# Holding ScalarE's weight casts and exponentials behind product copies and query squares in a two-layer attention and pooling block

## The chip, the cores and the metric

The kernel runs on one core of a Trainium2 chip. The metric is the device time of one execution in microseconds (us). Kernels are compared as medians of runs on the same chip. A profile of one execution gives the span, from the first instruction to the last, and what each engine did in it: PE is TensorE (matmuls), PEld its weight loads, DVE is VectorE, ACT is ScalarE, POOL is GpSimd, SP is SyncE, which here only issues DMAs.

## The reference

Two layers of the same block over 528 tokens (16 learned ones ahead of 512) of width 1024, in fp32, batch 1. Cut to what matters:

```python
def hybrid_layer(x, norm_g, w_in, ..., w_a, w_b, w_out, cos, sin, k_top):
    h = rms_norm(x, norm_g)
    proj = jnp.einsum('btd,de->bte', h, w_in)
    q, k, v, gate_a, u_b, gate_b, q_idx, k_idx, w_idx, merge = jnp.split(...)
    q = apply_rope(rms_norm(q...), cos_h, sin_h)        # k too; q_idx, k_idx: rope alone
    attn = indexer_sparse_attention(q, k, v, q_idx, k_idx, w_idx, k_top)
    y_a = jnp.einsum('bte,ed->btd', attn * jax.nn.silu(gate_a), w_a)
    pooled = multiscale_pool(u_b, pool_w, pool_b, pool_s)
    y_b = jnp.einsum('bte,ed->btd', pooled * jax.nn.silu(gate_b), w_b)
    g_a, g_b = jnp.split(jax.nn.sigmoid(merge), 2, axis=-1)
    return x + jnp.einsum('btd,de->bte', g_a * y_a + g_b * y_b, w_out)
```

The attention has 8 heads of 64 over one key and value head. For each query an index score picks the 128 best of the keys that its chunk may see, and a softmax runs over these alone. The output is the last 512 tokens after both layers.

## The kernel before

**Products in split fp32.** A weight matrix and an activation matrix are each split into a high part, rounded to the matmul type `fp32r`, and a low part, the rest. A product takes three passes on TensorE: high by high, high by low and low by high. Weights come in 54 chunks (27 a layer), mostly of 256 columns. SP loads each chunk as two halves into `raw` tiles (four buffers, so two chunks at a time), and each half is prepared into tiles `w` (eight buffers), in one of three ways:

- `high` and `low`: a ScalarE cast and a VectorE subtraction.
- `minus` and `plus` (the chunks in `by_dma`, lines 217 to 230): for the low part ScalarE writes the negated cast (L220), and a DMA from POOL's queue adds the raw weights to it in place (L221). The high part is another cast (L225). These are the chunks of the pools, the queries and `w_b` in each layer, and two of `w_out` in the last.
- `mixed_prep` (the chunks in `mixed`, lines 254 to 318): the ten gate chunks of each layer and the last two of `w_out`. Their products use seven multiplications of quarter blocks in place of eight, so the weights are first summed in blocks: `hi(n)` is a ScalarE cast (L264), `lo(n)` a VectorE subtraction (L267), and two DMAs on POOL's queue add blocks (L251, L278). Nine steps, `i0` to `i8`, make the seven operands `a12`, `a11`, `s2`, `s1`, `s3`, `s4`, `a22`.

**The order of the work.** TensorE and VectorE run in the order in which the code issues their instructions (`manual_schedule`). ScalarE, POOL and SP are ordered by the compiler's scheduler, which issues what it finds ready first; `tc.issue_after(ins)` forces what its block issues on the engine of `ins` to stand behind `ins` in that engine's order, with no wait for its end. Preparation steps wait in a queue: `group_done`, called after each group of matmuls, runs what is due and then one step, and `chunk()` runs all that are left before a chunk is used. In the mixed products `end()` runs them by a count, with a lead of five steps (`LEAD`) and nine steps for seven products; `NEEDS` gives the step that must be done before an operand's product.

**The places that the change touches.**

- `hi` puts its cast behind `mark[0]` where there is a mark. Before the change, only `rows` in the last stage sets one (L1483).
- `queries(g)` makes the query projection in four groups of 24 matmuls (128 tokens each, in a PSUM bank `d`, of which there are three). After a group, `q_post` issues two VectorE products for the rotation (tiles `t1`, `t2`), a ScalarE square for the norm (`sq`, L660), and a POOL addition (L669). The same `group_done` then runs the next preparation step, so `minus` of the next chunk is issued right after a square.
- `group_of_products` runs the seven products of a mixed chunk (12 matmuls each). `out` copies three of them from PSUM by ScalarE (`p1`, `u2`, `p5`, L1010). VectorE adds them to other products, and the bank of `p1` and `p5` is written again by a later product.
- `attention` runs beside the mixed products: `soft` computes on VectorE the logits and the minimum `mn`, and on ScalarE the exponential of each head (L782).
- In the last stage of layer 1 `rows` multiplies the first half of `w_out` by tokens, and `mix_out` runs the two mixed chunks of the second half, with `turned_out` to bring the results out.

Of the kernel before, what the change touches and what calls it, by code (L numbers as in the profile page):

```python
# [10 lines left out]
AF = mybir.ActivationFunctionType  # L11
# [9 lines left out]
HD = 64  # L21
# [70 lines left out]
def tile_block(ctx: ExitStack, tc: tile.TileContext, x, meta, w_in, pool_w, w_a, w_b, w_out, rows, hgain, c_tab, out):  # L92
    nc = tc.nc
    act, gp = nc.scalar, nc.gpsimd
# [20 lines left out]
    chunks = []  # L115
# [22 lines left out]
    raws, ready = {}, {}  # L138
# [37 lines left out]
    def w_prep_enqueue(casts_first=False, after=None):  # L176
        c = W["prep"]
        if c >= len(chunks):
            return
        W["prep"] += 1  # L180
        kt = chunks[c][0][0].shape[1]
        cols = 2048 // kt
        if c in plain:
            return
        ready[c] = {}
        if c in mixed:
            prep_q.extend(mixed_prep(c))
            return
        parts = ready[c] = ([], [])

        def split(which):
            if c == kept_chunk:
                if which not in own:
                    own[which] = one.tile([128, KT, 256], F32R, tag=("Ahi", "Alo")[which], name="wo")
                i = len(parts[which])
                t = own[which][:, i:i + kt // 2, :]
            else:
                t = w_tile().rearrange("p (k e) -> p k e", e=cols)
            parts[which].extend(t[:, k] for k in range(kt // 2))
            return t  # L200

        his, own = {}, {}

        def high(s):
            his[s] = split(0)
            act.copy(his[s], raws[c][s])

        def low(s):
            dve.tensor_sub(split(1), raws[c][s], f(his[s]))
            if s == 1:  # L210
                del raws[c]
                w_load()

        def second():
            low(0)
            high(1)

        def minus(s):
            t = split(1)
            act.activation(t, raws[c][s], AF.Copy, scale=-1.0)  # L220
            gp.dma_start(t, raws[c][s], accum_op=OP.add)  # L221

        def plus(s):
            t = split(0)
            act.copy(t, raws[c][s])  # L225
            if s == 1:
                del raws[c]
                w_load()
                with tc.issue_after(added[0]):
                    first_sum(c + 1)  # L230

        def highs():
            with tc.issue_after(after) if after else nullcontext():
                high(0)
                high(1)

        if casts_first:
            prep_q.extend((highs, lambda: low(0), lambda: low(1)))
        elif c in by_dma:
            prep_q.extend((lambda: minus(0), lambda: minus(1), lambda: plus(0)))  # L240
            if c in metas:
                prep_q.append(lambda: meta_queries(metas[c], raws[c]))
            prep_q.append(lambda: plus(1))
        else:
            prep_q.extend((lambda: high(0), second, lambda: low(1)))

    added, mark = [None], [None]

    def first_sum(c):
        if c in mixed:  # L250
            gp.dma_start(raws[c][0][:, 1], raws[c][0][:, 0], accum_op=OP.add)  # L251

    def mixed_prep(c):

        r0, r1 = raws[c]
        blk = {"a11": r0[:, 0], "a21": r0[:, 1], "a12": r1[:, 0], "a22": r1[:, 1]}
        src = {"a11": "a11", "a12": "a12", "a22": "a22", "s3": "a21", "s2": "s2", "s1": "a11", "s4": "a12"}
        ops = ready[c]

        def hi(n):  # L260
            t = w_tile().rearrange("p (s k e) -> p s k e", s=2, k=4)
            ops[n] = t
            with tc.issue_after(mark[0]) if mark[0] else nullcontext():
                act.copy(t[:, 0], blk[src[n]])  # L264

        def lo(n):
            dve.tensor_sub(ops[n][:, 1], blk[src[n]], f(ops[n][:, 0]))  # L267

        def i0():
            hi("a12")  # L270
            hi("a11")

        def i1():
            lo("a12")
            blk["s2"] = tmp.tile([128, 544], F32, tag="L", name="s2", bufs=LB)[:, :512].rearrange(
                "p (k e) -> p k e", k=4)
            dve.tensor_add(blk["s2"], blk["a21"], blk["a22"])
            gp.dma_start(blk["a12"], blk["s2"], accum_op=OP.add)  # L278
            lo("a11")

        def i2():
            dve.tensor_sub(blk["a11"], blk["s2"], blk["a11"])

        def i3():
            hi("s2")

        def i4():
            lo("s2")
            hi("s1")

        def i5():
            lo("s1")
            hi("s3")

        def i6():
            lo("s3")
            hi("s4")
            first_sum(c + 1)

        def i7():  # L300
            lo("s4")
            hi("a22")

        def i8():
            lo("a22")
            del raws[c]
            w_load()

        def counted(fn):
            def item():  # L310
                fn()
                progress[c] += 1
            return item

        progress[c] = 0
        return [counted(fn) for fn in (i0, i1, i2, i3, i4, i5, i6, i7, i8)]
# [138 lines left out]
    NR = one.tile([128, 4, NH], F32, name="NR")  # L455
# [192 lines left out]
    def q_post(t, ps, normed, dst, g=0):  # L648
        s, m = TOK[t]
        p3 = ps[:m, :256].rearrange("p (h d) -> p h d", h=4)  # L650
        t1 = tmp.tile([128, HB], F32, tag="tt", name="t1", bufs=6)
        t2 = tmp.tile([128, HB], F32, tag="tt", name="t2", bufs=6)
        v1 = t1[:m, :256].rearrange("p (h d) -> p h d", h=4)
        C, S = (Cg[:m, t], Sg[:m, t]) if normed else (ctab[:m, t], stab[:m, t])
        dve.tensor_tensor(v1, p3, C[:, None, :].to_broadcast([m, 4, 64]), op=OP.mult)
        dve.tensor_tensor(t2[:m, :256].rearrange("p (h a d) -> p h a d", h=4, a=2), swapped(ps[:m, :256], 4),
                          S.rearrange("p (a d) -> p a d", a=2)[:, None, :, :].to_broadcast([m, 4, 2, 32]), op=OP.mult)
        if normed:
            sq = tmp.tile([128, HB], F32, tag="tt", name="sq", bufs=6)
            act.activation(sq[:m, :256], ps[:m, :256], AF.Square, scale=HD ** -0.5)  # L660
            ss = small(4, "ss4")
            rq = small(4, "rq")

        def norms():
            dve.tensor_reduce(ss[:m], sq[:m, :256].rearrange("p (h d) -> p h d", h=4), axis=AX.X, op=OP.add)
            inv_rms(rq[:m] if t == 0 else RQ[:, t - 1, 4 * g:4 * g + 4], ss[:m], dve)
        if normed and t == 0:
            norms()
        added[0] = gp.tensor_tensor(t1[:m, :256], t1[:m, :256], t2[:m, :256], op=OP.add).ins  # L669
        if normed:  # L670
            qs = tmp.tile([128, 544], F32R, tag="L", name="qs", bufs=LB)[:, :512].rearrange("p (h c) -> p h c", h=4)
        else:
            qs = tmp.tile([128, 4, 128], F32R, tag="P", name="qs", bufs=PB)

        def second():
            if normed and t == 0:
                dve.tensor_tensor(v1, v1, rq[:m, :, None].to_broadcast([m, 4, 64]), op=OP.mult)
            act.copy(qs[:m, :, 0:64], v1)
            if normed and t:
                norms()  # L680

        def third():
            dve.tensor_sub(qs[:m, :, 64:128], v1, f(qs[:m, :, 0:64]))

        def trans():
            tp = bank("a", F32R)
            for h in range(4):
                pe.transpose(tp[:, h * 128:h * 128 + m], qs[:m, h, :], identr[:m, :m])
            act.copy(dst, f(tp).rearrange("p (h c) -> p h c", h=4)[:, :, :m])
        later(second, 1)  # L690
        later(third, QN if normed else QI)
        later(trans, QN + 1 if normed else QI + 1)
# [55 lines left out]
    def attention(ensure, later_rate, on):  # L748
# [18 lines left out]
        def soft(u):  # L767
            i, j = divmod(u, 4)
            n = NK[i]
# [9 lines left out]
            dve.tensor_tensor(mn, mn, RQ[:, i, 2 * j:2 * j + 2], op=OP.mult)  # L779
            for hh in range(2):  # L780
                h = 2 * j + hh
                act.activation(L[hh][:, :n], L[hh][:, :n], AF.Exp, scale=NR[:, i, h:h + 1], bias=mn[:, hh:hh + 1],  # L782
                               accum_out=sm[:, hh:hh + 1])
            st[u] = L, sm

        def scale(u):
# [191 lines left out]
        return early, late, last_sum, operands  # L978

    ROLES = [(0, 1, 2), (2, 0, 1), (1, 2, 0)]  # L980
    NEEDS = {"a11": 1, "a12": 2, "s2": 4, "s1": 5, "s3": 6, "s4": 7, "a22": 8}

    def group_of_products(r, base, n2, operands, total, direct, mid=None):

# [22 lines left out]

        def out(ps, name):
            o = sheet(n2, name)[:, :n2]
            act.copy(o, ps[:, :n2])  # L1010
            return o

        product(U, "a11", True)
# [552 lines left out]
```

## Time and profile before

| | |
|---|---|
| time, median of 3 runs | 745.1 us (743.18 to 748.33) |
| the profiled execution's own time | 743.89 us |
| its span | 742.1 us |
| granted TensorE clock | 1.0 |
| DMA | 106.42 MB, 143 GB/s on average |

A row of the profile names the source line, the engine, the operation, what is written and read (`out<-in`), the shapes, and times. TensorE's and VectorE's instructions are all recorded by one helper and stand under L63, so there the tiles' names tell them apart: `d`, `a` and `v` are PSUM banks, `w` prepared weights, `raw` staged ones. In a row of the timeline the first number is the start in us from the span's start and the second the duration; `x` counts the instructions merged into the row, and a bracket gives the engine's idle time before it and what ended that. In a row of waits stand the total in us, how many there were, and the longest.

### The profile page before, as it was taken

The numbers are of one execution on the slowest core, as the hardware profiler recorded it, in microseconds if no ns is written. First come the engines' busy times: TensorE is split into PE (matmuls) and PEld (weight loads), VectorE is DVE, ScalarE is ACT, GpSimd is POOL, SyncE is SP. The second block draws the span as 40 slices with busy tenths as digits, with TensorE's granted clock in tenths as the row PEclk, the third lists the DMA queues.
The fourth block names the chain that finished last, engine by engine and source line by source line (L and its number), as shares of the span: only waits on it lengthen the run. The fifth ranks groups of instructions, "written<-read, shape, count | busy, mean of one in ns | idle before, by whom it ended". The sixth has DMA issues, their size and how long they took to land.

```text
span 742.1 us, 16064 instructions
## 1 busy us (share of the span) xinstructions
PE 732.4 (99%) x5949; PEld 705.6 (95%) x5949; DVE 589.4 (79%) x1500; ACT 480.8 (65%) x1099; POOL 242.6 (33%) x320
## 2 busy tenths in 40 slices
PE   8999999999999999999999999999999999999997
PEld 7999998999999999999999989998899999999997
DVE  6866999999897775894358668999989878668773
ACT  6769735657788785543245796367578878865642
POOL 3742174721221210163256411755031221106300
PEclk9999999999999999999999999999999999999999
DMA  8766764864554532633422687569464644448832
GB/s 265 231 170 162 166 145 114 225 147 100 139 119 116 127 74 85 213 118 124 135 88 86 175 179 194 150 142 201 99 159 100 160 97 93 122 116 250 197 85 69
DMA packets 103567, 106.42 MB, mean 143 GB/s; under 512 B 5008, under 2 KB 83632, under 8 KB 103488
## 3 DMA queue, kind: packets, MB, share of 16 engines
q1 hardware_dynamic: 91888, 74.89, 33.3%
q0 software_dynamic: 11520, 30.41, 22.9%
q8 instruction: 47, 0.77, 0.4%
q14 instruction: 32, 0.26, 0.1%
q10 hardware_dynamic: 80, 0.08, 0.0%
HBM read 66.41 MB, written 8.55 MB: 101 GB/s over the span
## 4 chain that ended last, share of the span: by engine, by line
PE 69%; DVE 20%; ACT 3%; DMA 2%; issue 2%; POOL 2%; SPq 1%; DVEq 0%; POOLq 0%; ACTq 0%
PE d L63 56%; PE a L63 9%; DVE sc L63 6%; PE v L63 4%; DVE m L63 4%; DVE t L63 2%; DMA xt<-in_x_dram 2%; DVE w L63 1%; DVE nf L63 1%; DVE silb L63 1%; DVE us L63 1%; DVE mlo L63 1%; ACT w L225 1%; DVE qs L63 1%; ACT lt L782 1%
## 5 line engine op out<-in xcount | busy, mean ns | idle before, releaser
L63 PE MATMUL d<-hhi,w 128*128 128x256 f32 (+3 forms) x1392 | 278.3, 291 | 0.5 <-ACT p L1010 0.5
L63 PEld LDWEIGHTS d<-hhi,w 128*128 128x128 f32 x1392 | 222.3, 188 | 3.6 <-ACT p L1010 0.7
L63 PE MATMUL d<-hlo,w 128*128 128x256 f32 (+3 forms) x696 | 189.8, 289 | 0.0
L63 PEld LDWEIGHTS d<-hlo,w 128*128 128x128 f32 x696 | 131.3, 189 | 1.4 <-issue 0.2
L63 DVE TENSOR_TENSOR w<-raw,w 128x512 fp32r<-128x512 f32 (+1 forms) x156 | 120.6, 784 | 6.5 <-ACT w L264 6.3
L63 PE MATMUL d<-hsum,w 128*128 128x264 f32 (+1 forms) x720 | 95.7, 285 | 0.4 <-ACT u L1010 0.3
L63 PEld LDWEIGHTS d<-hsum,w 128*128 128x128 f32 x720 | 89.6, 188 | 1.5 <-ACT u L1010 0.5
L63 PE MATMUL d<-w,hhi 128*128 128x256 f32 x576 | 86.2, 287 | 0.7 <-ACT sq L660 0.7
L264 ACT CAST w<-raw 128x512 fp32r<-128x512 f32 x132 | 77.0, 622 | 5.9 <-DMA raw<-s 3.2
L63 PEld LDWEIGHTS d<-w,hhi 128*128 128x128 f32 x576 | 74.7, 188 | 5.2 <-issue 2.3
L251 POOL DMA_DIRECT2D raw<-raw x22 | 19.9, 903 | 114.6 <-DMA raw<-in_w_in_dram 43.3
L221 POOL DMA_DIRECT2D w<-raw x34 | 31.5, 944 | 73.8 <-ACT w L220 51.1
L63 DVE MATCH_REPLACE8 sc<-m,sc 128x400 f32<-128x400 f32 (+2 forms) x100 | 54.4, 547 | 0.0
L63 DVE MAX8 m<-sc 128x8 f32<-128x400 f32 (+2 forms) x100 | 53.1, 556 | 0.9
L782 ACT ACTIVATE lt<-lt,mn,NR 128x144 f32<-128x144 f32 (+3 forms) x64 | 42.2, 663 | 14.2 <-DVE mn L63 13.9
L278 POOL DMA_DIRECT2D raw<-s x22 | 19.2, 871 | 90.8 <-DVE s L63 51.2
L63 DVE SCALAR_TENSOR_TENSOR sc<-r,wsg,sc 128x144 f32<-128x144 f32 (+3 forms) x56 | 32.4, 581 | 17.4 <-ACT r L706 15.0
L63 PE MATMUL d<-w,hlo 128*128 128x256 f32 x288 | 45.5, 281 | 0.0
L63 PE MATMUL d<-mhi,w 128*128 128x272 f32 (+2 forms) x192 | 45.3, 324 | 0.0
L669 POOL TENSOR_TENSOR t<-t,t 128x256 f32<-128x256 f32 (+1 forms) x34 | 32.5, 956 | 26.4 <-DVE t L63 25.0
L1411 POOL TENSOR_TENSOR hlo<-ta,hhi 128x256 fp32r<-128x256 f32 (+1 forms) x28 | 26.8, 967 | 43.6 <-PE d L63 31.4
L706 ACT ACTIVATE r<-a,wab 128x272 f32<-128x272 f32 (+2 forms) x80 | 35.7, 495 | 5.9 <-PE a L63 5.9
(245 smaller groups left out, 1548.3 us busy)
## 6 DMA issues: line engine op xcount, KB each, us to landing
raw<-in_w_in_dram SPq DMA_DIRECT2D x88, 256.0 KB, 3.4
w<-raw POOLq DMA_DIRECT2D x34, 512.0 KB, 5.9
raw<-in_w_in_dram SPq DMA_DIRECT2D x32, 512.0 KB, 4.3
raw<-in_w_out_dram SPq DMA_DIRECT2D x12, 512.0 KB, 4.0
raw<-raw POOLq DMA_DIRECT2D x22, 256.0 KB, 4.0
raw<-s POOLq DMA_DIRECT2D x22, 256.0 KB, 3.3
kept<-res SPq DMA_DIRECT2D x16, 264.0 KB, 4.7
res<-kept SPq DMA_DIRECT2D x16, 264.0 KB, 5.9
```

Of the source, the lines that this page charges most:

```text
L63: return fn(*a, **k)
L221: gp.dma_start(t, raws[c][s], accum_op=OP.add)
L225: act.copy(t, raws[c][s])
L251: gp.dma_start(raws[c][0][:, 1], raws[c][0][:, 0], accum_op=OP.add)
L264: act.copy(t[:, 0], blk[src[n]])
L278: gp.dma_start(blk["a12"], blk["s2"], accum_op=OP.add)
L669: added[0] = gp.tensor_tensor(t1[:m, :256], t1[:m, :256], t2[:m, :256], op=OP.add).ins
L706: act.activation(r[:, n - 1::-1] if i == 0 else r[:, o:o + e], ps[:, :e], AF.Relu, scale=wab[:, i, h:h + 1])
L782: act.activation(L[hh][:, :n], L[hh][:, :n], AF.Exp, scale=NR[:, i, h:h + 1], bias=mn[:, hh:hh + 1], accum_out=sm[:, hh:hh + 1])
L1411: pool_end = gp.tensor_sub(hlo[:, j, a:a + n], d, f(hhi[:, j, a:a + n]))
```

## The change

Three things are edited. `mark[0]` is now also set by the square of a query group (L660) and by each product copy (L1010). The casts of `minus` and the exponentials of `soft` are put behind the latest mark, as the casts of `hi` were already; the casts of `plus`, and of `high`, are not. And for the last chunk of all, `hi("a11")` and `lo("a11")` are issued one step later each, with `NEEDS["a11"]` raised from 1 to 2 for every chunk.

```diff
         def minus(s):
             t = split(1)
-            act.activation(t, raws[c][s], AF.Copy, scale=-1.0)
+            with marked():
+                act.activation(t, raws[c][s], AF.Copy, scale=-1.0)
             gp.dma_start(t, raws[c][s], accum_op=OP.add)
...
+    def marked():
+
+        return tc.issue_after(mark[0]) if mark[0] else nullcontext()
...
+        soon = c <= len(chunks) - 2
 
         def hi(n):
             t = w_tile().rearrange("p (s k e) -> p s k e", s=2, k=4)
             ops[n] = t
-            with tc.issue_after(mark[0]) if mark[0] else nullcontext():
+            with marked():
                 act.copy(t[:, 0], blk[src[n]])
...
         def i0():
             hi("a12")
-            hi("a11")
+            if soon:
+                hi("a11")
...
             gp.dma_start(blk["a12"], blk["s2"], accum_op=OP.add)
-            lo("a11")
+            (lo if soon else hi)("a11")
 
         def i2():
+            if not soon:
+                lo("a11")
             dve.tensor_sub(blk["a11"], blk["s2"], blk["a11"])
...
-            act.activation(sq[:m, :256], ps[:m, :256], AF.Square, scale=HD ** -0.5)
+            mark[0] = act.activation(sq[:m, :256], ps[:m, :256], AF.Square, scale=HD ** -0.5).ins
...
-                act.activation(L[hh][:, :n], L[hh][:, :n], AF.Exp, scale=NR[:, i, h:h + 1], bias=mn[:, hh:hh + 1],
-                               accum_out=sm[:, hh:hh + 1])
+                with marked():
+                    act.activation(L[hh][:, :n], L[hh][:, :n], AF.Exp, scale=NR[:, i, h:h + 1], bias=mn[:, hh:hh + 1],
+                                   accum_out=sm[:, hh:hh + 1])
...
-    NEEDS = {"a11": 1, "a12": 2, "s2": 4, "s1": 5, "s3": 6, "s4": 7, "a22": 8}
+    NEEDS = {"a11": 2, "a12": 2, "s2": 4, "s1": 5, "s3": 6, "s4": 7, "a22": 8}
...
             o = sheet(n2, name)[:, :n2]
-            act.copy(o, ps[:, :n2])
+            mark[0] = act.copy(o, ps[:, :n2]).ins
             return o
```

## The prediction

> **What bounds the kernel now.** I read the page first (busy time, the chain of waits), then TensorE's waits, then the busy time by stage, and last the rows of ScalarE, TensorE and the DMA issues around the places that the change touches.
>
> ```profile
> span 742.1 us, 16064 instructions
> ...
> PE 732.4 (99%) x5949; PEld 705.6 (95%) x5949; DVE 589.4 (79%) x1500; ACT 480.8 (65%) x1099; POOL 242.6 (33%) x320
> ...
> PE 69%; DVE 20%; ACT 3%; DMA 2%; issue 2%; POOL 2%; SPq 1%; DVEq 0%; POOLq 0%; ACTq 0%
> ```
>
> TensorE is busy for 732.4 of 742.1 us. ScalarE, the engine that the change reorders, holds 3% of the chain. So the change can win only what TensorE now waits, and it loses whatever new wait it makes for TensorE. TensorE's waits, in total, times and longest:
>
> ```profile
> PE d L63 <- DVE ss L63: 1.5, 1, 1.5
> PE d L63 <- ACT p L1010: 1.2, 2, 0.7
> PE d L63 <- ACT sq L660: 0.7, 1, 0.7
> PE a L63 <- DVE res L63: 0.7, 1, 0.7
> PE a L63 <- DVE qs L63: 0.6, 1, 0.6
> PE d L63 <- ACT u L1010: 0.3, 1, 0.3
> ```
>
> These six make 5.0 us, 0.7% of the run. That is about all that can be won. The stages (length; busy time of PE, PEld, DVE, ACT, POOL; clock; DMA): queries and branch b of layer 0, its mixed products, and the same two of layer 1.
>
> ```profile
> 112.00:171.00 59.00, 58.30 (x488) 54.95 (x488) 57.66 (x153) 37.27 (x80) 26.66 (x31) 1.00 0.66 158
> 171.00:309.00 138.00, 137.48 (x1194) 134.27 (x1193) 110.85 (x305) 105.81 (x261) 24.79 (x41) 1.00 0.48 113
> 482.00:534.00 52.00, 51.31 (x338) 45.36 (x337) 51.72 (x133) 32.77 (x60) 23.25 (x27) 1.00 0.70 158
> 534.00:668.00 134.00, 133.47 (x1187) 130.50 (x1187) 108.50 (x297) 103.74 (x257) 27.28 (x41) 1.00 0.50 117
> ```
>
> In the two query stages VectorE is full (57.66 of 59, 51.72 of 52) and so runs behind TensorE; in the two mixed stages no helper is full.
>
> **The change part by part.** *What is moved.* PE and DVE keep the order of the code; ScalarE's order is chosen by the scheduler, which now puts a weight cast wherever its input is ready. I went through ScalarE's rows and asked which casts and exponentials run ahead of a square (L660) or product copy (L1010) that the code issues before them. There are 99: 13 casts of `minus` (L220), 84 of `hi` (L264) and 2 exponentials, from the first of these rows to the second:
>
> ```profile
> 112.81 2.00 ACT L220 ACTIVATE w<-raw 128x1024 fp32r<-128x1024 f32 x2
> ```
> ```profile
> 727.30 0.63 ACT L264 CAST w<-raw 128x512 fp32r<-128x512 f32 x1
> ```
>
> All 99 must now come later. The other 62 exponentials stand behind their mark already, so that part is nearly empty. `NEEDS["a11"]` of 2 binds only where a group begins with fewer than three steps done; the mixed groups begin with at least five done and the output group with three, so it costs nothing.
>
> *The casts of `minus` in the queries.* Each such cast is followed by an accumulating DMA on POOL's queue that makes the low half of the weights, and TensorE needs that in the third pass of the next chunk. So what is moved is cast plus DMA. The square waits for VectorE's rotation product of the same bank, hence for an engine that lags.
>
> ```profile
> 126.59 0.39 ACT L660 ACTIVATE sq<-d 128x256 f32<-128x256 f32 x1 [1.91 <-DVE t L63]
> ```
> ```profile
> 129.41 1.05 ACT L220 ACTIVATE w<-raw 128x1024 fp32r<-128x1024 f32 x1
> 130.37 0.36 ACT L660 ACTIVATE sq<-d 128x256 f32<-128x256 f32 x1
> ```
> ```profile
> 142.33 0.39 ACT L660 ACTIVATE sq<-d 128x256 f32<-128x256 f32 x1
> ```
> ```profile
> 145.93 0.79 PE L63 MATMUL d<-mhi,w 128*128 128x272 f32 x5
> ```
> ```profile
> DMA to landing us min/median/max: 4.5/5.9/9.9
> ```
>
> The cast at 129.41 is the second half for the first chunk of `w_b`. The code issues it behind the second square of the second `queries`, which ran at 142.33. So: 142.33 + 0.39 + 1.05 = 143.8 for the cast's end, + 5.9 for the DMA (last row: issue to landing of L221's) = 149.7. TensorE reads that half in the third matmul of the row at 145.93, at 146.2. It would stand still for **3.5 us**. With the shortest landing it is 2.1, with the longest 7.5; I take the median, since this stage's DMA share is 0.66. The chunk before it, behind the square at 126.59, lands at 126.59 + 0.39 + 1.05 + 5.9 = 133.9, a few tenths after its use; that delay is contained in the 3.5, since VectorE's lag does not grow with it.
>
> Behind the DMA issue POOL's rotation adds and powers are queued; they wait at most for one cast (1.05), and VectorE's lag covers that.
>
> [...]
>
> *The same in layer 1.*
>
> ```profile
> 492.61 0.39 ACT L660 ACTIVATE sq<-d 128x256 f32<-128x256 f32 x1 [0.52 <-DVE t L63]
> ```
> ```profile
> 496.97 1.11 PE L63 MATMUL d<-w,hhi 128*128 128x256 f32 x8
> ```
> ```profile
> 501.89 0.52 PE L63 MATMUL a<-identr,qs 128*128 128x128 f32 x4 [0.61 <-DVE qs L63]
> ```
>
> Here the second `queries` chunk is the tight one: 492.61 + 0.39 + 1.05 + 5.9 = 499.95. TensorE needs it in the fifth of the eight matmuls at 496.97, four at 0.12 later: 497.45. That is 2.5 us (1.1 to 6.5). Soon after TensorE waits 0.6 for VectorE; being late, it waits that less. Net **1.9 us** (0.5 to 5.9).
>
> *The casts of `hi` in the products.*
>
> ```profile
> 189.53 0.36 ACT L1010 COPY p<-d 128x264 f32<-128x264 f32 x1
> ```
> ```profile
> 189.94 0.40 PE L63 MATMUL d<-hhi,w 128*128 128x264 f32 x1 [0.49 <-ACT p L1010]
> ```
> ```profile
> 726.25 0.62 ACT L264 CAST w<-raw 128x512 fp32r<-128x512 f32 x1 [1.34 <-DMA raw<-s]
> 726.77 0.37 ACT L1010 COPY p<-d 128x256 f32<-128x256 f32 x1
> ```
> ```profile
> 727.19 1.57 PE L63 MATMUL d<-osum,w 128*128 128x256 f32 x11 [0.73 <-ACT p L1010]
> ```
>
> At 726.25 a hoisted cast waits for a DMA, the copy of the product stands behind it, and TensorE waits 0.73 for the copy; at 189.53 two exponentials and a cast are ahead. Both waits go: **-1.2**. Of the 0.7 for the square at 130.37, the bank is also read by this VectorE row:
>
> ```profile
> 129.53 0.41 DVE L63 TENSOR_TENSOR t<-d,Sg 128x256 f32<-128x256 f32 x1
> ```
>
> It ends at 129.94, so the square can gain only some 0.3: **-0.3**.
>
> What a held cast costs: its low half on VectorE comes later. VectorE waits for these casts now
>
> ```profile
>   DVE w L63: 7.6, 8
> ```
>
> 7.6 us in eight waits, and TensorE's list has no row for `w`. The weights are used two or more products later (a product is twelve matmuls, 1.5 us), so I take **+0.5**; the ends are zero (a later cast makes no low half earlier, as VectorE's order is fixed) and another 7.6. The cover is the lead of five steps; ScalarE's 32 idle us in 138 leave room to catch up.
>
> *The former order in the last group.*
>
> ```profile
> 721.37 0.68 DVE L63 TENSOR_TENSOR w<-raw,w 128x512 fp32r<-128x512 f32 x1
> ```
> ```profile
> 723.00 0.41 PE L63 MATMUL a<-consts,res 128*128 128x128 f32 x2 [0.67 <-DVE res L63]
> ```
>
> The low half at 721.37 moves behind the sums for which TensorE then waits 0.67. They come 0.68 sooner: **-0.6**. Next late is the low half itself, needed in the following product's third matmul; that is why not the whole 0.67.
>
> *Sum:* 3.5 + 1.9 + 0.5 - 1.2 - 0.3 - 0.6 = +3.8 us. The profiled execution took 743.9 (span 742.1), 1.2 under the median of the runs. Forecast: 745.1 + 3.8 = **748.9**, +0.5%.
>
> **The rivals.** *The held DMAs stay covered (no stall).* Then -2.1 + 0.5 remains: 743.5. It needs the DMA to land within 2.4 us of the cast, or the squares to come two us sooner. For it: ScalarE is emptier ahead of the squares. Against: no landing under 4.5, and the squares hang on VectorE. [...]
>
> *Slower: the staging buffers come free late and SP's queue stands.*
>
> ```profile
> 141.60 1.79 SPq L946 DMA_DIRECT2D hsheet<-far  x2
> ```
> ```profile
> 151.63 1.21 ACT L952 CAST hhi<-hsheet 128x528 fp32r<-128x528 f32 x2
> ```
>
> SP's fetch of the sums follows in its queue on the load of a later chunk, and that load needs the buffer that the late accumulate reads. The fetch would go at 149.7 in place of 141.60 and land at 155 or so (the 4.5 and the issue); the ScalarE cast that stands at 151.63 would wait 3.4, with the copies of TensorE's banks behind it. It decides where TensorE isn't late itself by as much. Twice 3.4 on top of the forecast: 755.7.
>
> *Slower: ScalarE idles before each copy and crowds after it,* so that VectorE's waits for casts double and all of it reaches TensorE: +7.6 for the 0.5: 756.0. For: 84 moved casts. Against: the idle quarter of ScalarE, and two products of lead.
>
> *Faster by over 1%:* all five us of waits gone, and more that no row names. 739.6 is not yet 1%.
>
> **How the numbers follow.** Some 1% is what a measurement of this kernel tells from no change: 737.6 to 752.6. Forecast 0.50 (its own range 745 to 753; 0.06 of it above 752.6); covered 0.20; SP's queue 0.15 and crowding 0.10 (0.19 of these above); over 1% faster 0.05. So faster 0.05, same 0.70, slower 0.25. The range from 741 to 757 leaves out the fast case and the far ends of both slow ones.
>
> **What would show it.** Right: in the profile after, TensorE waits for a DMA of `w<-raw` near 146 and 497, a few us each; L220's rows stand behind the squares; no wait of TensorE for `p` at 189 and 727 nor for `res` near 722. Wrong: no wait on `w<-raw` (then the covered rival); TensorE waiting for `zb` copies with ScalarE held by `hsheet` (SP's queue); waits on `lt` or `w` in the mixed stages (crowding).

## The result, and the profile after

| | before | after |
|---|---|---|
| median | 745.09 us (743.18 to 748.33, 6 runs) | 752.33 us (751.0 to 753.2, 6 runs) |
| ratio | | 1.0095, 95% interval [1.007, 1.012] |
| the profiled execution, its span | 743.89, 742.1 us | 753.2, 751.4 us |

The changed kernel is slower by 7.2 us. The forecast was +3.8 and lay on the right side; the size was half of what came.

After's page (span, busy time, shares of the chain of waits):

```profile
span 751.4 us, 16106 instructions
...
PE 735.3 (98%) x5949; PEld 707.1 (94%) x5949; DVE 592.5 (79%) x1500; ACT 482.2 (64%) x1099; POOL 243.5 (32%) x320
...
PE 68%; DVE 18%; DMA 5%; ACT 5%; POOL 2%; issue 2%; SPq 1%; DVEq 0%; POOLq 0%; ACTq 0%
```

The counted work of the five engines is the same, to the instruction (the 42 more of the total are not among it). ScalarE went from 3% of the chain to 5% and the DMA from 2% to 5%. After's waits of TensorE (us in total, times, longest):

```profile
PE d L63 <- ACT w L226: 4.5, 4, 2.0
PE d L63 <- DMA w<-raw: 1.9, 3, 1.0
PE a L63 <- DMA xt<-in_x_dram: 1.7, 2, 1.5
PE d L63 <- DVE ss L63: 1.5, 1, 1.5
PE d L63 <- DVE c L63: 0.8, 1, 0.8
PE d L63 <- ACT sq L669: 0.4, 1, 0.4
PE a L63 <- DVE qs L63: 0.3, 1, 0.3
PE a L63 <- ACT KI L652: 0.3, 1, 0.3
PE a L63 <- DVE res L63: 0.2, 1, 0.2
```

Two rows are new and large: 4.5 us on the casts of `plus` (L226 here, L225 before) and 1.9 on the DMA behind `minus`. Both waits for `p` have gone, `sq` fell from 0.7 to 0.4 and `res` from 0.7 to 0.2. The wait for `xt` is the input's load in the first 20 us. It comes and goes between the profiled executions (1.7 us here, 1.2 to 1.4 in experiments 1, 2 and 6, none before and in the other four) and has no part in the change.

TensorE issues the same matmuls in the same order in both kernels, so its delay can be read matmul by matmul. These are the places where it grew or shrank (before's time axis):

| place | added us | what TensorE waits for after |
|---|---|---|
| 18.3, start | +1.5 | load of `xt` |
| 128.6, 130.8 | +0.5, -0.3 | VectorE's `qs`; (part of the wait for the square gone) |
| 131.4, `queries`, layer 0 | +1.6 | cast of `plus` |
| 131.9 to 133.4 | +1.5 | nothing: its granted clock is 0.50 |
| 145.4 and 146.2, first `w_b` chunk | +2.3, +0.5 | cast of `plus`, then the DMA |
| 189.9, 196.7 | -0.6, -0.3 | (wait for `p` gone) |
| 203.4, 286 | +0.9, +0.3 | VectorE's `c` at the first |
| 491 to 497.45, `queries`, layer 1 | +0.4, +0.6, +0.9, +1.3 | `us`, casts of `plus`, DMA |
| 501.9, 511.7 | -0.7, -0.3 | (VectorE's lag takes up some) |
| 523.6, 539, `w_b`, layer 1 | +0.8, -0.4 | the DMA |
| 723.0, 727.2 | -0.5, -0.8 | (waits for `res` and `p` gone) |

Layer 0's query stage and `w_b` cost 1.6 + 2.3 + 0.5 = 4.4, layer 1's 2.6, together 7.0; the places of the other parts bring -1.0; the start and the clock add 1.5 each. With the 0.2 of the second row that is 9.2 of the 9.3 us between the two profiled executions.

### The profile page after: what moved, and what is told of

Same layout as the page of the kernel before. It is cut to its first block, busy times and chain, and to the rows that moved or that the text cites. A ratio compares the mean times of both kernels' runs of the same rounds, so it can differ in the third digit from the quotient of the medians.

```text
span 751.4 us, 16106 instructions
## 1 busy us (share of the span) xinstructions
PE 735.3 (98%) x5949; PEld 707.1 (94%) x5949; DVE 592.5 (79%) x1500; ACT 482.2 (64%) x1099; POOL 243.5 (32%) x320
## 4 chain that ended last, share of the span: by engine, by line
PE 68%; DVE 18%; DMA 5%; ACT 5%; POOL 2%; issue 2%; SPq 1%; DVEq 0%; POOLq 0%; ACTq 0%
PE d L63 55%; PE a L63 9%; DVE sc L63 4%; PE v L63 4%; DVE m L63 3%; DMA w<-raw 2%; DVE w L63 2%; DMA xt<-in_x_dram 2%; DVE t L63 2%; ACT lt L792 1%; DVE lt L63 1%; ACT w L226 1%; DVE us L63 1%; POOL t L678 1%; DVE silb L63 1%
## 5 line engine op out<-in xcount | busy, mean ns | idle before, releaser
L63 PEld LDWEIGHTS d<-hlo,w 128*128 128x128 f32 x696 | 131.4, 189 | 1.3 <-issue 0.2
L63 PE MATMUL d<-w,hhi 128*128 128x256 f32 x576 | 87.8, 290 | 3.8 <-ACT w L226 2.4
L270 ACT CAST w<-raw 128x512 fp32r<-128x512 f32 x132 | 78.6, 622 | 3.2 <-DMA raw<-s 2.0
L222 POOL DMA_DIRECT2D w<-raw x34 | 31.9, 955 | 67.0 <-ACT w L221 41.2
L807 POOL TENSOR_SCALAR pm<-lt,rs 128x16 f32<-128x16 f32 x48 | 24.4, 542 | 47.3 <-DVE rs L63 47.3
```

Of the source, the lines that this page charges most:

```text
L63: return fn(*a, **k)
L807: (gp if j < 3 else dve).tensor_scalar(pms[i][:, 2 * j + hh, :], L[hh][:, 0:16], rs[:, hh:hh + 1], None, op0=OP.mult)
```

## The experiments

All times are medians beside the kernel before on the same chip: 744.69 us (28 runs) for the first four kernels, 744.22 us (17 runs) for the last three. Steps of the kind tabled above are given for the profiled executions.

**1. The change without its hold on `minus`.**

```diff
         def minus(s):
             t = split(1)
-            with marked():
-                act.activation(t, raws[c][s], AF.Copy, scale=-1.0)
+            act.activation(t, raws[c][s], AF.Copy, scale=-1.0)
```

> The changed kernel with the hold on the casts of minus taken away; casts of hi and exponentials stay held, the last group keeps its new order. Theory Q (all of the loss is in the two query stages, from the held casts of minus): no wait of TensorE for high casts (plus) or for the DMAs of w<-raw there, and the gains elsewhere stand alone: 743.2 us (742 to 744.5), some 9 under the changed kernel's 752.3. Rival M (held casts crowd ScalarE in the mixed products, VectorE's waits for casts of hi rose from 6.5 to 21.6 us and that costs): 748 or more.

743.62 us (742.92 to 745.19), ratio 0.9978 [0.9963, 0.9994]. Both new rows are gone from TensorE's waits. The whole loss hangs on the hold on `minus`; without it the rest of the change gains 1.1 us.

**2. The hold on `minus` alone.**

```diff
-            act.activation(t, raws[c][s], AF.Copy, scale=-1.0)
+            with tc.issue_after(square[0]) if square[0] else nullcontext():
+                act.activation(t, raws[c][s], AF.Copy, scale=-1.0)
...
-            act.activation(sq[:m, :256], ps[:m, :256], AF.Square, scale=HD ** -0.5)
+            square[0] = act.activation(sq[:m, :256], ps[:m, :256], AF.Square, scale=HD ** -0.5).ins
```

> The kernel before with one edit: the casts of minus held behind the squares of queries. Theory Q: the whole loss and the losses alone: 752.5 to 754.5 us, TensorE waiting for casts of plus at the start of chunks (about 4.5 us in 4 waits) and for w<-raw (about 2), and in some executions a TensorE clock under 1. Rival M: under 749. Rival D (only the late DMA costs, as the prediction had it, not the casts of plus): waits for w<-raw of 5 us and none for plus.

752.99 us (751.92 to 756.07), ratio 1.0117 [1.0096, 1.0139]. Its waits of TensorE:

```profile
PE d L63 <- ACT w L226: 4.5, 4, 2.0
PE d L63 <- DMA w<-raw: 1.8, 3, 1.0
...
PE d L63 <- ACT p L1011: 1.2, 2, 0.7
PE a L63 <- DVE res L63: 0.7, 1, 0.7
PE d L63 <- ACT sq L661: 0.4, 1, 0.4
```

The two rows of the loss are here as in the changed kernel, while `p` and `res` still wait as before: the parts act each at its own place. The gain at the square (0.7 to 0.4) belongs to this part.

**3. The marks of the product copies alone** (`hi` behind L1010, no other part).

```diff
-            act.copy(o, ps[:, :n2])
+            mark[0] = act.copy(o, ps[:, :n2]).ins
```

> The kernel before with one edit: product copies set the mark, so that the casts of hi are held behind them. Theory Q: TensorE's two waits for p (1.2 us) go, VectorE's waits for casts rise to about 20 us and cost TensorE nothing: 744.0 (743 to 745). Rival M: 748 or more.

744.01 us (743.44 to 745.24), ratio 0.999 [0.998, 1.0], so the gain of 0.7 is not clear of noise. VectorE's waits for these casts rose from 7.6 to 22.3 us. Here is what is left of the gain in the first mixed group, in TensorE's timeline, and VectorE's add that frees the bank (`c`), first in the kernel before and then in this one:

```profile
203.15 0.39 PE L63 MATMUL d<-hhi,w 128*128 128x264 f32 x1 [0.74 <-DVE c L63]
```
```profile
202.81 0.41 DVE L63 TENSOR_TENSOR c<-d,p 128x264 f32<-128x264 f32 x1
```
```profile
202.68 0.41 DVE L63 TENSOR_TENSOR c<-d,p 128x264 f32<-128x264 f32 x1
```

0.8 us is won at 189.9 and 0.3 at 196.7, and 0.9 goes back at 203.4, where there was no wait before; at 727.2 another 0.7 is won. VectorE's order is fixed. On its way to this add it got 0.6 us sooner, as `p` came earlier, and lost 0.6 again: some 0.4 at low halves of weights that wait for held casts (187.2 and 190.2) and 0.25 at a step that waits for ScalarE (200.0). So `c` runs when it ran before, and TensorE, 0.9 sooner by then, waits for it. In the changed kernel the same wait is 0.8.

**4. The later `a11` in the last group alone** (`soon` and `NEEDS`).

```diff
         def i0():
             hi("a12")
-            hi("a11")
+            if soon:
+                hi("a11")
...
-            lo("a11")
+            (lo if soon else hi)("a11")
 
         def i2():
+            if not soon:
+                lo("a11")
```

> The kernel before with one edit: in the last chunk a11 is prepared one step later and NEEDS of a11 is 2. Both theories: TensorE's wait of 0.67 for res near 722 falls to 0.2, -0.5 us: 744.6 (744.0 to 745.2). If the prediction's sizing was wrong and the low half of a11 becomes late: 745 or more with a wait for w after 723.

743.29 us (741.83 to 743.91), ratio 0.9979 [0.9968, 0.999]: more than expected, and the lowest median of this study, though the interval of experiment 1 overlaps this one. TensorE gains 0.6 at the wait for `res` and 0.8 at the wait for `p`, though no cast is held. ScalarE and TensorE in this kernel:

```profile
723.04 1.14 ACT L265 CAST w<-raw 128x512 fp32r<-128x512 f32 x2 [0.34 <-DVE raw L63]
724.08 0.36 ACT L1014 COPY p<-d 128x256 f32<-128x256 f32 x1
```
```profile
725.25 2.99 PE L63 MATMUL d<-osum,w 128*128 128x256 f32 x24
```

With the later `a11` the scheduler does not put the cast that waits for a DMA ahead of the copy, so the copy ends at 724.4 and the matmul at 725.25 has no bracket.

**5. The hold on the exponentials alone.**

```diff
+                with tc.issue_after(held[0]):
+                    act.activation(L[hh][:, :n], L[hh][:, :n], AF.Exp, scale=NR[:, i, h:h + 1], bias=mn[:, hh:hh + 1],
+                                   accum_out=sm[:, hh:hh + 1])
```

(`held[0]` is set by the squares and the product copies.)

> The kernel before with the hold on the exponentials alone (behind squares and product copies). The prediction counts 2 of 64 exponentials that run ahead of their mark, so it expects no change: within 0.5 us of the kernel before. Rival: the exponentials were what stood ahead of the copy `p` in the first mixed group (two of them and a cast), so this hold alone takes TensorE's wait for `p` near 190 us and wins some 0.5 to 0.8 us.

743.93 us (743.28 to 746.66), ratio 0.9998 [0.9984, 1.0013]. No change in time; TensorE still waits 0.9 for `p` in two waits. By itself this part wins nothing, as the count of two rows said, but half of the rival came in: the wait near 190 is gone with this hold alone, and in its place one comes at 196.6, where the copy stands behind a cast that waits for a DMA.

```profile
195.66 0.62 ACT L264 CAST w<-raw 128x512 fp32r<-128x512 f32 x1 [0.92 <-DMA raw<-s]
196.18 0.37 ACT L1011 COPY p<-d 128x264 f32<-128x264 f32 x1
```
```profile
196.61 1.72 PE L63 MATMUL d<-hsum,w 128*128 128x264 f32 x12 [0.77 <-ACT p L1011]
```

**6. The changed kernel with the high casts ahead.** `plus(s)` is now called at the start of `minus(s)`, ahead of the held cast; the step that frees the raw buffers stays where it was.

```diff
         def minus(s):
+            plus(s)
             t = split(1)
             with marked():
                 act.activation(t, raws[c][s], AF.Copy, scale=-1.0)
...
-            prep_q.extend((lambda: minus(0), lambda: minus(1), lambda: plus(0)))
+            prep_q.extend((lambda: minus(0), lambda: minus(1), lambda: None))
...
-            prep_q.append(lambda: plus(1))
+            prep_q.append(freed)
```

> The changed kernel, with each half's high cast issued by the code just ahead of its own held `minus` cast, so that it takes its buffer from the ring of `w` before the held one. Theory of the buffer ring: the high casts of the first pass are late only because a held cast ahead of them has the earlier place in the ring; then TensorE's 4.5 us of waits for `ACT w` fall to under 1, the waits for the DMA into `w` stay at 2 to 3, and the time is 748 to 750. Rival: ScalarE itself is too busy behind the squares; then the waits for `ACT w` stay above 3 and the time stays at 752.

756.12 us (752.11 to 757.85), ratio 1.0142 [1.0115, 1.0168]. One of the three things expected came in: the waits for `plus` vanished, so ScalarE had room for these casts. But the other row rose from 1.9 to 6.9, and the time rose too:

```profile
PE d L63 <- DMA w<-raw: 6.9, 4, 3.1
```
```profile
143.51 0.39 ACT L671 ACTIVATE sq<-d 128x256 f32<-128x256 f32 x1
143.79 1.06 ACT L222 ACTIVATE w<-raw 128x1024 fp32r<-128x1024 f32 x1
```
```profile
145.14 0.92 POOL L223 DMA_DIRECT2D w<-raw  x1 [0.40 <-ACT w L222]
```
```profile
150.55 0.63 PE L63 MATMUL d<-mhi,w 128*128 128x272 f32 x3 [3.07 <-DMA w<-raw]
...
507.14 0.74 PE L63 MATMUL d<-w,hhi 128*128 128x256 f32 x4 [1.75 <-DMA w<-raw]
...
533.92 0.96 PE L63 MATMUL d<-mhi,w 128*128 128x512 f32 x3 [1.50 <-DMA w<-raw]
```

The square, the cast, POOL's issue and TensorE 5.4 us after it: this is the chain that the prediction laid out, bare. In the changed kernel TensorE stands first for the high cast and then reaches the low half when it has nearly landed. The two waits lie in front of each other and not side by side, so taking the first away uncovers the second. That the median is even longer goes along with the clock: all six runs had a granted clock of 0.993 to 0.998 (last section). The two at 0.998 took 752.4 on average, about what the changed kernel takes, the four at 0.993 to 0.995 took 756.0 to 757.9. No run separates the two.

**7. The changed kernel with `minus` held in layer 0 alone.**

```diff
-            with marked():
+            with marked() if c < len(chunks) // 2 else nullcontext():
                 act.activation(t, raws[c][s], AF.Copy, scale=-1.0)
```

> The changed kernel, with the `minus` casts held in layer 0 alone and free in layer 1. Theory: the costs of the two layers add. In the changed kernel's trace layer 0 lost 1.6, 2.3 and 0.5 us at its steps, and some 1.5 more in executions where TensorE's clock halved; layer 1 lost 3.2 and got 1.0 back. So 743.6 (no `minus` cast held) + 4.4 = 748.0, up to 749.5 with the clock. Rival, the sizes of the prediction (3.5 and 1.9): 743.6 + 3.5 = 747.1, and layer 1 would hold 5 of the 8.7 us. Rival, VectorE's lag takes up one layer's loss: 744 to 746.

749.58 us (747.69 to 751.84), ratio 1.0074 [1.0052, 1.0097], just above the 749.5 expected at most. The two runs at a clock of 1.0 took 748.2 on average, 4.6 above the kernel of experiment 1 against the 4.4 that the theory of adding costs gave. Waits of TensorE:

```profile
PE d L63 <- ACT w L226: 3.4, 2, 2.0
...
PE d L63 <- DMA w<-raw: 0.2, 1, 0.2
```

From here to the changed kernel's runs at 1.0 (751.2 on average) layer 1 adds 3.0. The three kernels were not timed together: taken each against the kernel before beside it (744.69, 744.22, 745.09), the shares are 5.1 and 2.2. Either way each layer has a loss of its own, and neither takes up the other's.

## Why the prediction was right in direction and short in size

**The DMA behind `minus`, layer 0 (+3.5): the mechanism and the size hold, where it stands alone.** Experiment 6 shows it: TensorE had lost 1.1 us before this place, so its square at 143.51 is 142.4 on before's axis (predicted 142.33, which is before's own), the landing at 150.5 is 149.4 (predicted 149.7), and the delay added there is 3.3. The median of the landings was close to the right value; the shortest would have given 2.1. The shortest, median and longest landing of the changed kernel's DMAs of this kind (its L222, 512 KB each):

```profile
DMA to landing us min/median/max: 4.5/5.6/8.1
```

None landed under 4.5.

In the changed kernel itself little of this wait was left to see. The prediction's sign of being right, a few us each on `w<-raw` near 146 and 497, came in as 0.2 and 1.0:

```profile
508.43 0.75 PE L63 MATMUL d<-w,hhi 128*128 128x256 f32 x4 [1.01 <-DMA w<-raw]
```

**The step that failed: "TensorE needs that in the third pass of the next chunk. So what is moved is cast plus DMA".** The step counted only what the diff holds. ScalarE's rows of the changed kernel show that more came late:

```profile
128.53 0.38 ACT L669 ACTIVATE sq<-d 128x256 f32<-128x256 f32 x1 [1.91 <-DVE t L63]
128.81 1.05 ACT L221 ACTIVATE w<-raw 128x1024 fp32r<-128x1024 f32 x1
129.76 1.04 ACT L226 CAST w<-raw 128x1024 fp32r<-128x1024 f32 x1
...
133.48 1.04 ACT L226 CAST w<-raw 128x1024 fp32r<-128x1024 f32 x1
...
146.51 0.38 ACT L669 ACTIVATE sq<-d 128x256 f32<-128x256 f32 x1 [1.91 <-DVE t L63]
146.79 1.05 ACT L221 ACTIVATE w<-raw 128x1024 fp32r<-128x1024 f32 x1
...
148.20 1.06 ACT L226 CAST w<-raw 128x1024 fp32r<-128x1024 f32 x1
...
151.36 1.04 ACT L226 CAST w<-raw 128x1024 fp32r<-128x1024 f32 x1
```

and TensorE's:

```profile
134.57 0.91 PE L63 MATMUL d<-w,hhi 128*128 128x256 f32 x4 [1.41 <-ACT w L226]
...
152.46 0.39 PE L63 MATMUL d<-mhi,w 128*128 128x272 f32 x1 [2.04 <-ACT w L226]
...
153.68 0.62 PE L63 MATMUL d<-mhi,w 128*128 128x272 f32 x3 [0.20 <-DMA w<-raw]
```

The casts of `plus` carry no mark, and the change does not name them. They follow the held `minus` in the code, write tiles of the same ring of eight `w` buffers, and now run behind it. TensorE needs them in the first pass, and starts 0.05 us and 0.06 us after the second one of each chunk ends. Experiment 6 shows that their place behind the held cast is what makes them late: put ahead of it in the code, they are never waited for. That the ring is the tie, buffers being given out in code order, fits the code but was not tried by itself.

This was furthest from the forecast in the chunk before. The prediction let its delay be "contained in the 3.5, since VectorE's lag does not grow with it". The changed kernel loses 1.6 there to a high cast and 2.8 more at `w_b`, 4.4 in all.

**Layer 1 (+1.9, net): too small.** In experiment 6 the predicted stall at the fifth of eight matmuls measured 2.0 (predicted 2.5) with 0.7 taken up at `qs` (predicted 0.6). What was left out is `w_b` of this layer: another 1.5 of stall there, 0.7 in the changed kernel. All of layer 1 measured 2.6 in the changed kernel's trace.

**The held `hi` casts (+0.5 - 1.2 - 0.3): half of the 1.2 was won and lost again, and one term stood under the wrong part.** VectorE's waits for casts did not double but tripled, from 7.6 us in 8 to

```profile
DVE w L63 <- ACT w L270: 22.5, 25, 2.4
```

and TensorE lost little by it: the wait of 0.8 at 203.4 takes back what was won at 189.9 and 196.7, and +0.3 stands at 286. This fits the cover that the prediction named, the lead of five steps, though no run varied the lead; it also stands against the crowding rival's price. The wait for `p` at 189.9 did go with the hold, but its worth went back at 203.4; the one at 727.2 goes without the hold too (experiment 4). The 0.3 at the square came as predicted, from the hold on `minus`, with 0.5 lost just ahead of it at 128.6.

**The later `a11`, which the prediction calls the former order (-0.6): half of its worth.** It measured -1.4 alone, since it takes the wait for `p` at 727.2 too. In the changed kernel both parts reach for the same wait, so their gains (0.7 and 1.4) do not add: with both and the empty part on the exponentials, experiment 1 has 1.1.

**SP's queue (the rival of 755.7): its first half happened, its price was nothing.** The fetch of the sums moved from 141.60 by 9.7 us, where TensorE itself was 4.8 late (1.5 + 0.2 + 1.6 + 1.5):

```profile
151.33 1.43 SPq L956 DMA_DIRECT2D hsheet<-far  x2
```
```profile
ACT hhi L962 <- DMA hsheet<-far: 4.0, 1, 4.0
```

and ScalarE waited 4.0 us for it (second row, from the waits). Yet no wait of TensorE for a copy `zb` came of it.

**The sum.** At the granted clock of 1.0 the changed kernel takes 751.2, that is +6.1 on 745.1; the table has 7.0 for the two layers' `minus` and -1.0 for the rest. Predicted were 3.5 + 1.9 and -1.6. The half clock, in three of six runs, lifts the median by another 1.1. That 5.4 for `minus` came as near to 7.0 as it did is in part luck: the DMA's waits, priced at 3.5 and 2.5, were 1.9 in all, 0.7 of it at a place without a price, and the casts of `plus`, priced at nothing, took 4.5 in their place.

## What to carry to other kernels

When one operation is held back, list what the scheduler has to place behind it: what the code issues after it into the same ring of buffers may come later too, as the casts of `plus` did here, and what counts is the consumer that needs any of these first. Two waits on the same matmuls are not a sum; the later one shows only what the earlier one leaves (here 4.5 and 1.9 us together, and 6.9 for the second when the first was gone), so a repair of the first may give nothing. And take a change with several parts apart: here the smallest edit, two steps in another order, was worth 1.4 us, while the hold that looked like the main part cost 7.

## What the runs showed of the hardware

TensorE's granted clock fell from 1.00 to 0.50 behind a stall of 1.41 us in the changed kernel, and behind one of 3.07 us in experiment 6. It stayed at 1.00 behind one of 2.04 us in the changed kernel, and behind the stall of 1.42 us in experiment 2 that stands at the same matmul as the 1.41. So the length of the stall alone did not decide. In the changed kernel's clock record the entries up to TensorE's last matmuls stand at 5.28, 134.99 and 138.40 us, the second and third 38 and 39 times 3.413 us behind the first; in the record of the kernel before there is one, at 5.94. Here are busy time of PE, PEld, DVE, ACT and POOL, the granted clock and the DMA's share in pairs of stretches of 3.41 us: for the changed kernel around the stall of 1.41 us and around that of 2.04 us, for experiment 2 around that of 1.42 us, and for experiment 6 around that of 3.07 us. The changed kernel's lie whole numbers of 3.413 us behind its first entry.

```profile
131.57:134.99 3.42, 1.60 (x17) 0.95 (x8) 3.39 (x12) 2.68 (x6) 2.61 (x4) 1.00 1.01 163
134.99:138.40 3.41, 3.41 (x18) 3.41 (x17) 3.38 (x10) 1.18 (x4) 0.69 (x1) 0.50 0.78 287
148.64:152.05 3.41, 1.77 (x16) 1.55 (x14) 3.38 (x12) 3.07 (x7) 2.15 (x3) 1.00 0.84 131
152.05:155.47 3.42, 2.81 (x20) 2.51 (x20) 3.39 (x12) 1.59 (x5) 1.73 (x2) 1.00 0.99 265
```
```profile
132.84:136.25 3.41, 2.04 (x17) 2.04 (x18) 3.38 (x11) 2.97 (x7) 1.73 (x2) 1.00 0.89 211
136.25:139.66 3.41, 3.41 (x32) 3.25 (x31) 3.38 (x12) 1.57 (x4) 1.44 (x2) 1.00 0.56 154
```
```profile
147.71:151.13 3.42, 0.58 (x4) 0.58 (x5) 3.39 (x11) 0.43 (x2) 1.72 (x3) 1.00 0.99 187
151.13:154.54 3.41, 3.41 (x21) 3.16 (x19) 1.12 (x4) 1.21 (x4) 1.02 (x2) 0.50 1.11 340
```

In both cases the clock stands at 0.50 for 3.41 us, and in the changed kernel TensorE lost about 1.5 us there (the table's fourth row). The two halvings follow stretches in which TensorE was busy for 1.60 and 0.58 us. Behind every other such stretch of the changed kernel up to TensorE's last matmuls the clock stayed at 1.00, the least busy being the one with 1.77; in the kernel before the least busy has 2.68, and the clock stayed at 1.00 throughout. In experiment 2 the stretch that holds the stall has 2.04 as it is laid here; laid from 131.20 to 134.61 it has 1.59. That where the stall falls in such stretches decides is the author's reading of these cases: two halvings are few, and how many busy microseconds are enough was not shown. The halving shows in the mean clock of a run: 3.41 us at half in 751 is 0.002. The changed kernel's runs at 1.0 took 751.0 to 751.5, those at 0.995 to 0.998 took 753.1 to 753.2; of the 24 runs of the four kernels that hold `minus`, 15 stand at 0.998 or less, of the 90 runs of the others beside them 7. That the stalls cause the halving is read from these stretches and this count; no run turned one on by itself.
